# One core, a two-block network with 16 experts: layer 1's memory keys ahead of the experts, the memory's norm vector in its weights, expert products interleaved, the overflow branch at the end

## The chip, the cores and the metric

One Trainium2 chip, one core of it. A core has a matrix engine (PE, or TensorE), a vector engine (DVE), an activation engine (ACT), a general engine (POOL, or GpSimd) and a queue engine (SP), which here issues nearly all transfers. The metric is the time of one launch on the device in microseconds (us). Everything is float32, from inputs in HBM to the output in HBM.

## The reference, cut to what matters

```python
# first block: 256 tokens of 1024 features
x = layer_norm(alpha * x + (1 + gt1) * hybrid_mixer(h), ln1_g, ln1_b)
h = layer_norm(x) * (1 + sc2) + sh2
...
# experts: one group of 4 by softmax, the best 2 of its 4 experts
for e in range(16):
    hid = silu(t @ w_gate[e]) * (t @ w_up[e])          # 1024 -> 512
    out = out + gates[:, e:e + 1] * (hid @ w_down[e])  # 512 -> 1024
x = layer_norm(alpha * x + (1 + gt2) * out, ln2_g, ln2_b)
# second block, for l in (0, 1): mixer with w_in, cross-attention, feed-forward
x = x + mixer(rmsnorm(x, norm_mix[l]), ...)
x = x + cross_attn(rmsnorm(x, norm_xattn[l]), rmsnorm(mem, norm_mem[l]), w_xq[l], w_xkv[l], w_xo[l])
x = x + ffn(rmsnorm(x, norm_ffn[l]), ...)

def rmsnorm(x, g): return x * rsqrt(mean(x ** 2) + 1e-6) * g
def cross_attn(hx, hm, w_q, w_kv, w_o):
    q = hx @ w_q
    k, v = hm @ w_kv          # first 512 columns keys, last 512 values
    ...
```

The keys and values of the memory depend on `mem`, `norm_mem[l]` and `w_xkv[l]` alone, so they can be computed anywhere in the program.

## The kernel before, in words

**Products.** Weights stream from HBM in blocks of 1 MB into a ring of 6 buffers (`raw`, L114 to L117). For most products a block is then split into a high part `whi` (ACT, L140) and a low part `wlo` (DVE, or another engine that the list `loeng` names, L140 and L141), in rings `hi` and `lo` of 4 half-blocks each, and `mm3` (L163 to L165) makes three matmuls of each pair. `linA` gives tokens by features in `psA` (128x512 matmuls), `linB` features by tokens in `psB` (128x256). `featT` (L228, L249) transposes an activation on PE and splits it, on ACT (high) and DVE (low). Expert products take their weights unsplit, as single matmuls.

**Memory.** `memT(l)` (L1720) loads `mem_2`, normalises it (`normT`, L296: multiply by the row's factor `memr` and by the vector `gn` on DVE, L294), and transposes it. `keys(l)` (L1734) and `values(l)` (L1741) multiply with the two halves of `w_xkv_2[l]`. Where they stand in the program: keys(0) at the very start (L445), values(0) within the router (L1185), keys(1) behind the last expert (L1304), values(1) as `filler` between the layer norm at the experts' end and the second block.

**Router and dispatch.** From x, PE, DVE and ACT compute the logits, the chosen experts and each token's rank in its expert (`moe`, L1083; logits and ranks to L1181). Each expert has 64 slots. The gathers (L1191 to L1196) bring the tokens into slot order with 128x512 matmuls.

**Experts.** They are taken in 8 pairs q (L1258 to L1295). For a pair, `half(q, 0)` and `half(q, 1)` (matmul at L1244) make gate and up into one PSUM bank each, the two experts on 64 partitions each; `hid` is formed on ACT and DVE (L1273, L1274), transposed on PE (`pth`, L1283), copied to SBUF by ACT (`hx`, L1285) and multiplied with the down weights (`yg`, L1292). PE's order in a pair is: gate, up, the combine of the pair before (L1375 to L1383: `evac` L1251 on DVE and L228, then `pco` matmuls L1381 and L1382, then an addition into `acc`), the transposes, down. A pair takes 12 weight blocks of 1 MB, 96 in all. The string `CHUNKS` says in which ring each block lands, r for a raw buffer and h for a hi and a lo buffer (the blocks named `wx` in the profile).

**Overflow.** Tokens beyond 64 slots would be handled in a body behind a branch (`overflow`, L1317): every engine loads the count (L1321, TENSOR_LOAD) and branches (L1322). With these inputs the body is skipped. It stands ahead of pair 4.

**Behind the experts** come the last combine with the layer norm's statistics (`lnstat`, L314), `lngb` (the layer norm with gain and bias, L322 to L341; its `rsq` runs on POOL, L257 and L259), the norm and the transposes of x for the second block (L294, L249, L228), and the first products with `w_in_2`.

**Order.** A tile scheduler sets waits from the tiles' use; the order on each engine is that of the program text, except where `with self.after(...)` ties a piece to an instruction.

Of the kernel before, what the change touches and what calls it, by code (L numbers as in the profile page):

```python
# [40 lines left out]
_add("stri", (_i[:, None] < _i[None, :]))  # L41
_add("iota", np.broadcast_to(_i, (P, P)))
# [6 lines left out]
_add("gidx", np.broadcast_to(np.array([0.0, 1.0, 2.0, 3.0]), (P, 4)))  # L49
# [16 lines left out]
class Build:  # L66
    PAGES = {4: 21, 2: 7, 1: 5}
# [99 lines left out]
    def linA(self, x, KT, W, n0, n, r=None, inturn=False, tag="lin"):  # L167
# [5 lines left out]
        for k0 in range(0, KT, kb):  # L173
            kk = min(kb, KT - k0)
            w = self.wblk(W[k0 * P:(k0 + kk) * P, n0:n0 + n].rearrange("(k p) n -> p k n", p=P), kk, n, r)
# [136 lines left out]

    def lnstat(self, st, n, x):
# [77 lines left out]
    def attn(self, qk, V, out, first=True, nsink=None, gate=None, swa=False):  # L391
# [4 lines left out]
        mk = lambda m, n: m.rearrange("p (a b) -> p a b", a=4)[:, 0:n, :]  # L396
        PTs = {}
        for i, heads in ((0, (0, 1, 2, 3)), (1, (0, 1)), (1, (2, 3))):
# [4 lines left out]
            if swa and i == 1:  # L403
                nc.tensor.matmul(S[:, :, 0:P], self.identb, self.smaskb.rearrange("p (a b) -> p a b", a=2), start=False, stop=False,
# [33 lines left out]
    def run(self):  # L438
        nc, tc, A = self.nc, self.tc, self.A
        with tc.tile_pool(name="cst", bufs=1) as self.cp, tc.tile_pool(name="w", bufs=2) as self.wp, \  # L440
# [4 lines left out]
            mT = self.memT(0)  # L445
# [22 lines left out]
    def setup(self):  # L468
# [44 lines left out]
    def setup2(self):  # L513
# [6 lines left out]
        self.tri, self.stri, self.iota = self.C("tri"), self.C("stri"), self.C("iota")  # L520
# [30 lines left out]
    def setup3(self):  # L551
        nc, cp = self.nc, self.cp
        mp, rr, r1, rd, d8 = self.late
        b16 = cp.tile([P, 11 * P], BF, name="b16")
        nc.vector.tensor_copy(b16[:, 0:P], self.ident)
        self.identb = b16[:, 0:P]
        o = P
        for i, (m, n) in enumerate((("cmask", 4), ("smask", 2), ("dmask", 4))):
            v = b16[:, o:o + n * P]
            nc.vector.tensor_copy(v.rearrange("p (a b) -> p a b", a=n), bc(mp[:, i * P:(i + 1) * P], 1, n))  # L560
            setattr(self, m + "b", v)
            o += n * P
# [16 lines left out]
    def ropetables(self):  # L579
# [4 lines left out]
        ang = self.small([P, 2, 48], "ang", 1)  # L584
        for t in range(2):
            nc.vector.tensor_scalar(ang[:, t, :], C("invf"), pf[:, t:t + 1], None, op0=ALU.mult)
        k = self.small([P, 2, 48], "kk", 1)
# [11 lines left out]
        sn = self.small([P, 2, 48], "sn", 1)  # L599
# [13 lines left out]
        self.rt = rt  # L613

# [468 lines left out]
    def moe(self):  # L1083
# [174 lines left out]
        for q in range(8):  # L1258
# [8 lines left out]
            elif q < 4:  # L1267
                gather(1, 2 * q - 2)
# [619 lines left out]
```

## Time and profile before

| | us |
|---|---|
| three runs | 1710.87, 1709.19, 1705.22 (median 1709.19) |
| profiled execution | 1710.13, of it span 1708.4 |
| PE busy in the span | 1604.0 (94%) |
| DVE busy | 991.7 (58%) |
| ACT busy | 737.3 (43%) |
| POOL busy | 236.6 (14%) |
| HBM, mean over the span | 198 GB/s |

Times inside the execution are counted from the span's start. In the span, the first mixer ends at about 350 us, the layer norm, router and dispatch last to about 399, the 8 pairs of experts to about 651, and the second block's first product with `w_in_2` begins at about 688. The rows further down are of the views that the prediction uses: the windows view gives for a stretch the busy time of each engine (with the instructions in brackets), the granted clock of TensorE as a share of full speed, the share of time that the transfer engines are busy, and GB/s. The timeline gives start, length, engine, source line, operation, output and inputs; in square brackets stands how long the engine was idle just before and what released it.

### The profile page before, as it was taken

The page shows a single profiled execution, that of the slowest core. Times are in us where ns is not written, and L with a number is a line of the kernel's source. Part 1 is how long each engine was busy: PE and PEld are TensorE (multiplying, and loading weights), DVE is VectorE, ACT ScalarE, POOL GpSimd, SP SyncE. Part 2 cuts the span into 40 slices and gives each one's busy share as a digit, 9 for nine tenths or more (in the row PEclk, how much of TensorE's full clock was granted, in tenths as well). Part 3 has the DMA queues.
Part 4 walks back from the last instruction along what each step waited for, and adds up shares of the span by engine and source line. Part 5 has one row for each costly group of instructions (what it writes and reads, how often), then busy time and mean ns, then how long its engine had stood idle before and what let it go on. Part 6 is the DMA issues. An engine that isn't in the chain of part 4 may idle for free. (4 is left out here: it accounts for less than half of the span.)

```text
span 1708.4 us, 23536 instructions
## 1 busy us (share of the span) xinstructions
PE 1604.0 (94%) x9272; PEld 1258.9 (74%) x9288; DVE 991.7 (58%) x1501; ACT 737.3 (43%) x1282; POOL 236.6 (14%) x262
## 2 busy tenths in 40 slices
PE   6599999988997898999999999999999999999998
PEld 5478988865432336877788789987877787789986
DVE  6857785772211217677746755544777647655544
ACT  3345764432110004565443544444565544544443
POOL 3498442440000002100000000000100000000000
PEclk9699999998998999999999999999999999999999
DMA  9867356645998997544156545654534155535550
GB/s 305 304 198 243 115 167 229 213 165 189 385 403 333 412 415 279 173 129 143 59 173 200 174 131 173 202 179 134 183 93 150 50 189 193 185 116 193 185 185 25
DMA packets 181318, 340.53 MB, mean 199 GB/s; under 512 B 20640, under 2 KB 96528, under 8 KB 173776
## 3 DMA queue, kind: packets, MB, share of 16 engines
q1 hardware_dynamic: 177072, 331.29, 55.9%
q0 software_dynamic: 1936, 6.52, 1.1%
q8 instruction: 76, 1.25, 0.3%
q10 hardware_dynamic: 2192, 1.12, 0.3%
q14 instruction: 42, 0.34, 0.1%
HBM read 337.86 MB, written 1.05 MB: 198 GB/s over the span
## 5 line engine op out<-in xcount | busy, mean ns | idle before, releaser
L141 DVE TENSOR_TENSOR wlo<-raw,whi 128x1024 fp32r<-128x1024 f32 (+3 forms) x368 | 451.5, 1238 | 315.1 <-ACT whi L140 314.3
L140 ACT CAST whi<-raw 128x1024 fp32r<-128x1024 f32 (+3 forms) x372 | 375.1, 1021 | 380.9 <-PE psA L165 148.8
L163 PE MATMUL psB<-hTh,whi 128*128 128x256 f32 x896 | 254.5, 284 | 0.5 <-ACT xbc L883 0.5
L165 PE MATMUL psB<-hTh,wlo 128*128 128x256 f32 x896 | 253.8, 283 | 0.8 <-DVE wlo L141 0.8
L164 PE MATMUL psB<-hTl,whi 128*128 128x256 f32 x896 | 254.2, 284 | 0.0
L163 PE MATMUL psA<-whi,hTh 128*128 128x512 f32 (+4 forms) x496 | 188.1, 380 | 2.6 <-ACT sg L976 1.9
L165 PE MATMUL psA<-whi,hTl 128*128 128x512 f32 (+4 forms) x496 | 187.4, 378 | 0.5 <-DVE hTl L228 0.5
L164 PE MATMUL psA<-wlo,hTh 128*128 128x512 f32 (+4 forms) x496 | 186.6, 376 | 0.0
L163 PEld LDWEIGHTS psB<-hTh,whi 128*128 128x128 f32 x896 | 171.7, 192 | 2.6 <-issue 1.1
L164 PEld LDWEIGHTS psB<-hTl,whi 128*128 128x128 f32 x896 | 171.7, 192 | 2.0 <-issue 1.9
L165 PEld LDWEIGHTS psB<-hTh,wlo 128*128 128x128 f32 x896 | 171.6, 192 | 1.7 <-DVE wlo L141 1.1
L1244 PE MATMUL pgu<-raw,xg 128*64 128x512 f32 x304 | 116.1, 603 | 0.0
L163 PEld LDWEIGHTS psA<-whi,hTh 128*128 128x128 f32 x496 | 93.8, 189 | 20.6 <-ACT sg L976 2.3
L165 PEld LDWEIGHTS psA<-whi,hTl 128*128 128x128 f32 x496 | 93.7, 189 | 18.9 <-issue 2.4
L164 PEld LDWEIGHTS psA<-wlo,hTh 128*128 128x128 f32 x496 | 93.7, 189 | 16.0 <-issue 0.7
L1244 PE MATMUL pgu<-wx,xg 128*64 128x512 f32 x208 | 94.9, 599 | 0.0
L363 ACT ACTIVATE pr<-S,nm 128x256 f32<-128x256 f32 (+1 forms) x160 | 66.4, 427 | 59.7 <-DVE nm L356 41.8
L638 POOL TENSOR_TENSOR macc<-macc,wmod 128x512 f32<-128x512 f32 x59 | 91.8, 1557 | 1.8
L164 PE MATMUL pd<-wlo,hhl 128*128 128x512 f32 x176 | 69.8, 397 | 0.0
L165 PE MATMUL pd<-whi,hhl 128*128 128x512 f32 x176 | 69.6, 395 | 0.0
L163 PE MATMUL pd<-whi,hhl 128*128 128x512 f32 x176 | 69.3, 395 | 0.0
L274 POOL TENSOR_SCALAR sse<-ssq 128x1 f32<-128x1 f32 x16 | 3.9, 242 | 443.8 <-ACT xn L272 432.1
(580 smaller groups left out, 3006.4 us busy)
## 6 DMA issues: line engine op xcount, KB each, us to landing
raw<-in_w_in SPq DMA_DIRECT2D x62, 1024.0 KB, 5.2
raw<-in_w_gate_up SPq DMA_DIRECT2D x44, 1024.0 KB, 5.1
raw<-in_w_down SPq DMA_DIRECT2D x42, 1024.0 KB, 6.1
wmod<-in_w_mod SPq DMA_DIRECT2D x48, 512.0 KB, 5.0
raw<-in_w_gate SPq DMA_DIRECT2D x19, 1024.0 KB, 8.3
raw<-in_w_up SPq DMA_DIRECT2D x19, 1024.0 KB, 10.5
wx<-in_w_gate SPq DMA_DIRECT2D x26, 512.0 KB, 8.7
wx<-in_w_up SPq DMA_DIRECT2D x26, 512.0 KB, 12.3
```

Of the source, the lines that this page charges most:

```text
L140: self.wsplits.append((self.nc.scalar.copy(hi, rv), self.loeng.pop(0).tensor_sub(lo, rv, hi.bitcast(F32)) if self.loeng else self.nc.vecto ...
L141: self.nc.vector.tensor_sub(lo, rv, hi.bitcast(F32))))
L163: m(out, l[0], r[0], start=start, stop=False)
L164: m(out, l[0], r[1], start=False, stop=False)
L165: self.lastmm = m(out, l[1], r[0], start=False, stop=stop)
L274: self.nc.gpsimd.tensor_scalar(sq[2], sq[1][:, 0:1], 1.0 / D, RMS_EPS, op0=ALU.mult, op1=ALU.add)
L363: le = nc.scalar.activation(pr[:, h, :], S[:, h, :], AF.Exp, bias=nm[:, h:h + 1], accum_out=den[:, h:h + 1])
L638: return e.tensor_add(acc, acc, w)
L1244: self.lastmm = nc.tensor.matmul(ps[i * 64:i * 64 + 64, :], x, w[i][k], start=kt == 0, stop=kt == 7, skip_group_check=True)
```

## The change

**Keys of layer 1.** `keys(1)` now stands right behind `values(0)`, before the first expert, on the same transposed memory; `loeng` is now DVE, DVE and four times POOL, so that four low parts run on POOL in place of two. At the end only `values(1)` is left as filler, and its weights are loaded and split ahead of the branch.

**Norm vector.** `memT` multiplies the memory by the row factor only (`scaledT`: one DVE operation per 128 rows). The vector `norm_mem` is loaded as a column, and `wblk` multiplies the raw weight block by it, block of 128 rows by block, on ACT and in place, ahead of the split.

**Experts.** `half` now makes half of a gate or up product. The next pair's first gate half goes in front of this pair's transposes, the second between `hx` and the down product. The gathers and `slots` for later pairs move with them. `CHUNKS` is now "rrrrrrhhhh".

**Branch.** The overflow branch is now behind the last combine, ahead of `values(1)` and the layer norm. Its body, if taken, recomputes the statistics.

**Small parts.** The rank uses `tri` in place of `stri`, the iota is 64 wide, the masks are kept once and broadcast in the matmul's operand, temporaries of the rope tables and of the softplus lie in pages, and one page more is reserved (`PAGES`).

```diff
-    def wblk(self, src, a, b, r=None, pages=None):
+    def wblk(self, src, a, b, r=None, pages=None, gain=None):
         r = self.raw(src, a, b) if r is None else r
+        if gain is not None:
+            for j in range(a):
+                self.nc.scalar.activation(r[:, j * b:(j + 1) * b], r[:, j * b:(j + 1) * b], AF.Copy, scale=gain[:, j:j + 1])
...
+    def scaledT(self, x, r, name):
+        xT = self.newT(8, name)
+        self.chain = []
+        for t in range(2):
+            self.nc.vector.tensor_scalar(x[t], x[t], r[t], None, op0=ALU.mult)
+            self.featT(x[t], 8, xT, t)
+            self.f(x[t])
+        return xT
...
+        nc.scalar.dma_start(cr[8:24, 0:P], A["norm_mem_2"].rearrange("l (a b) -> (l a) b", b=P))
...
-        nc.tensor.transpose(pt[:, 0:8], cr[0:8, 0:P], idt[:8, :8])
+        nc.tensor.transpose(pt[:, 0:24], cr[0:24, 0:P], idt[:24, :24])
+        self.memg = cp.tile([P, 16], F32, name="memg")
+        nc.scalar.copy(self.memg, pt[:, 8:24])
...
-    CHUNKS = "rrhrh"
+    CHUNKS = "rrrrrrhhhh"
...
-        self.loeng = [nc.vector, nc.vector, nc.gpsimd, nc.gpsimd]
+        self.loeng = [nc.vector, nc.vector] + [nc.gpsimd] * 4
         self.values(0, self.mT0)
+        self.keys(1, self.mT0)
...
-        late, ready = None, []
+        late = None
+        pg = self.bank("lin", "pg")
+        for c in range(2):
+            half(0, 0, c, pg)
+        slots(0)
         for q in range(8):
             if q == 4:
                 self.f(*Sp, *xh, *xl, *xgp[0])
-                ready += [[self.wchunk(wgu(0, 8 + i, c)) for i in range(2)] for c in range(2)]
-                self.overflow(oi, gov, acc)
-            pg = half(q, 0)
...
-            pu = half(q, 1)
-            if late:
-                self.combine(ST[(q - 1) // 4][:, (q - 1) % 4, :], evac(late), acc)
+            pu = self.bank("lin", "pu")
+            for c in range(2):
+                half(q, 1, c, pu)
             hid = self.a(2, "hid")
             nc.scalar.activation(hid, pg, AF.Silu)
             nc.vector.scalar_tensor_tensor(hid, hid, gs[:, q:q + 1], pu, op0=ALU.mult, op1=ALU.mult)
...
+            if late:
+                self.combine(ST[(q - 1) // 4][:, (q - 1) % 4, :], evac(late), acc)
+            if q < 7:
+                pg = self.bank("lin", "pg")
+                half(q + 1, 0, 0, pg)
             pt = v4(self.bank("m", "pth"))
...
             nc.scalar.copy(v4(hx), pt)
...
+            if q < 7:
+                half(q + 1, 0, 1, pg)
             y = [self.bank("S", f"yg{n}") for n in range(2)]
...
         with self.after(self.lastraw):
-            mT = self.memT(1)
-            w = self.wB(8, A["w_xkv_2"][1], 0)
+            mT = self.memT()
+            wv = self.wmem(1, 0, 512) + self.wmem(1, 1, 512)
         self.combine(ST[1][:, 3, :], evac(late), acc, st)
...
-        self.keys(1, mT, w)
+        self.overflow(oi, gov, acc, st)
 
         def filler():
-            self.values(1, mT)
+            self.values(1, mT, wv)
             self.freeT(mT)
```

The order of instructions shows at three places what this moves. On POOL, between the first mixer and the experts (`rsv` and `rs` are the layer norms' reciprocal roots, for which the scaling on DVE waits; `wlo` the low weight parts; the last rows are the router's), the order before was:

```order
L257 TENSOR_SCALAR rsv<-bmv 128x1
L259 TENSOR_TENSOR rs<-rsv,mhalf 128x1
L140 TENSOR_TENSOR wlo<-raw,whi 128x1024 x2
L257 TENSOR_SCALAR rsv<-bmv 128x1 x2
L259 TENSOR_TENSOR rs<-rsv,mhalf 128x1 x2
L1228 TENSOR_SCALAR acc_3460<-x_269 128x1024
L1116 TENSOR_TENSOR xnl_3175<-xn,xnh_3173 128x1024
L257 TENSOR_SCALAR rsv<-bmv 128x1
```

and with the change, where lines 138, 259 and 261 are the former 140, 257 and 259:

```order
L259 TENSOR_SCALAR rsv<-bmv 128x1
L261 TENSOR_TENSOR rs<-rsv,mhalf 128x1
L138 TENSOR_TENSOR wlo<-raw,whi 128x1024 x2
L259 TENSOR_SCALAR rsv<-bmv 128x1 x2
L138 TENSOR_TENSOR wlo<-raw,whi 128x1024
L261 TENSOR_TENSOR rs<-rsv,mhalf 128x1 x2
L138 TENSOR_TENSOR wlo<-raw,whi 128x1024
L259 TENSOR_SCALAR rsv<-bmv 128x1
L261 TENSOR_TENSOR rs<-rsv,mhalf 128x1
L1124 TENSOR_TENSOR xnl_3178<-xn,xnh_3176 128x1024
L1124 TENSOR_TENSOR xnl_3179<-xn,xnh_3177 128x1024
```

One low part has come between the second `rsv` and its `rs`, and one more ahead of the next `rsv`. On PE, from the end of up (`pgu`) to the start of down in a pair of experts, before:

```order
L1244 MATMUL pgu<-wx,xg_3407 64x512
L1244 MATMUL pgu<-raw,xg_3408 64x512
L1244 MATMUL pgu<-wx,xg_3408 64x512
L1244 MATMUL pgu<-raw,xg_3408 64x512
L1244 MATMUL pgu<-wx,xg_3408 64x512
L1283 MATMUL pth<-idt,hid 128x128 x4
L1292 MATMUL yg_6226<-raw,hx 64x512
L1292 MATMUL yg_6227<-raw,hx 64x512
```

and with the change (`pu` is this pair's up, `pg` the next pair's gate):

```order
L1251 MATMUL pu<-raw,xg_3556 64x512 x4
L1251 MATMUL pg<-wx,xg_3553 64x512
L1288 MATMUL pth<-idt,hid 128x128 x4
L1251 MATMUL pg<-wx,xg_3553 64x512 x3
L1251 MATMUL pg<-wx,xg_3554 64x512 x4
L1251 MATMUL pg<-wx,xg_3555 64x512 x4
L1251 MATMUL pg<-wx,xg_3556 64x512 x4
L1303 MATMUL yg_4320<-raw,hx 64x512
L1303 MATMUL yg_4321<-raw,hx 64x512
```

Nothing stood between up, the transposes and down; now one gate matmul stands ahead of the transposes and 15 ahead of down. On PE at the experts' end (`pco` is the last combine, `ptr` the transposes of the memory, `psB` keys(1)), before:

```order
L1381 MATMUL pco<-yh,ST_3459 128x512
L249 MATMUL ptr<-idt,xn 128x128 x8
L1381 MATMUL pco<-yh,ST_3459 128x512
L1382 MATMUL pco<-yl,ST_3459 128x512 x2
L249 MATMUL ptr<-idt,xn 128x128 x8
L163 MATMUL psB<-memTh_6388,whi 128x256
L164 MATMUL psB<-memTl_6389,whi 128x256
L165 MATMUL psB<-memTh_6388,wlo 128x256
```

and with the change:

```order
L1396 MATMUL pco<-yh,ST_3607 128x512
L251 MATMUL ptr<-idt,xn 128x128 x8
L1396 MATMUL pco<-yh,ST_3607 128x512
L1397 MATMUL pco<-yl,ST_3607 128x512 x2
L251 MATMUL ptr<-idt,xn 128x128 x8
L1396 MATMUL pco<-yh,ST_3607 128x512
L1397 MATMUL pco<-yl,ST_3607 128x512
L1396 MATMUL pco<-yh,ST_3607 128x512
L1397 MATMUL pco<-yl,ST_3607 128x512
L1333 TENSOR_LOAD oi
L1334 COMPARE_AND_BRANCH
```

Where keys(1) began there is now the branch, once the last combine is through, and values(1) begin behind it. On DVE the branch stands between the statistics of the last layer norm and their aggregate (L322 before), with one low part of a weight block behind it ahead of that; on SP the loads of the memory, of two blocks of `w_xkv_2`, of the gain and bias and of the first two blocks of `w_in_2` stand ahead of it.

## Rows read from the trace of the kernel before

**Rows 1.** Waits of PE, 398.7 to 650.7 us: total us, times, longest us.

```profile
PE pth L1283 <- DVE hid L1274: 5.6, 6, 0.9
PE yg L1292 <- ACT hx L1285: 4.1, 6, 0.7
PE pco L1382 <- issue: 3.0, 1, 3.0
```

**Rows 2.** Timeline of PE and DVE around the branch.

```profile
526.92 0.59 PE L1292 MATMUL yg<-wx,hx 128*64 128x512 f32 x1
...
532.26 1.22 PE L1381 MATMUL pco<-yh,ST 128*128 128x512 f32 x2 [4.75 <-ACT yh L228]
...
530.79 1.29 DVE L1251 TENSOR_TENSOR yf<-yg,gt 128x512 f32<-128x512 f32 x2 [11.90 <-PEq L1322]
```

**Rows 3.** Windows: us, busy of PE, PEld, DVE, ACT, POOL, PEclk, DMA share, GB/s.

```profile
527.50:541.00 13.50, 5.80 (x10) 2.12 (x9) 4.13 (x7) 1.14 (x2) 0.63 (x1) 0.67 1.02 414
541.00:650.70 109.70, 100.38 (x424) 35.70 (x423) 20.34 (x32) 8.37 (x14) 0.00 (x0) 0.98 0.99 397
...
540.00:560.00 20.00, 18.38 (x76) 6.25 (x76) 2.12 (x3) 1.18 (x2) 0.00 (x0) 0.93 0.86 322
...
600.00:620.00 20.00, 18.41 (x84) 6.37 (x86) 1.49 (x3) 1.18 (x2) 0.00 (x0) 1.00 1.02 416
```

**Rows 4.** SP's queue: first expert block behind ten prefetched ones, and the last.

```profile
408.81 1.17 SPq L117 DMA_DIRECT2D raw<-in_w_down  x2
...
631.10 0.33 SPq L117 DMA_DIRECT2D raw<-in_w_down  x1
```

**Rows 5.** Timeline of PE: a pair's down product.

```profile
616.17 3.66 PE L1292 MATMUL yg<-raw,hx 128*64 128x512 f32 x16 [0.68 <-ACT hx L1285]
```

**Rows 6.** Windows: the layer norm, router and gathers ahead of the experts.

```profile
350.00:398.70 48.70, 36.47 (x174) 29.89 (x172) 32.96 (x75) 13.48 (x22) 18.00 (x14) 0.83 0.41 147
```

**Rows 7.** Timeline of POOL and DVE at the first layer norm.

```profile
356.25 5.14 POOL L140 TENSOR_TENSOR wlo<-raw,whi 128x1024 fp32r<-128x1024 f32 x2
...
356.23 5.71 DVE L341 SCALAR_TENSOR_TENSOR x<-sg,rs,l1b 128x512 f32<-128x512 f32 x2 [0.47 <-POOL rs L259]
...
370.56 1.40 DVE L341 SCALAR_TENSOR_TENSOR x<-sg,rs,l1b 128x512 f32<-128x512 f32 x2
```

**Rows 8.** Timeline of PE: first and last of 46 matmuls in a row within keys(1).

```profile
667.73 0.28 PE L165 MATMUL psB<-memTh,wlo 128*128 128x256 f32 x1
...
672.98 0.28 PE L165 MATMUL psB<-memTh,wlo 128*128 128x256 f32 x1
```

**Rows 9.** Timeline of PE: last down product, first matmul of the second block.

```profile
650.15 0.59 PE L1292 MATMUL yg<-raw,hx 128*64 128x512 f32 x1
...
687.55 0.34 PE L163 MATMUL psA<-whi,hTh 128*128 128x384 f32 x1
```

**Rows 10.** Timeline of DVE between these two.

```profile
663.96 1.28 DVE L314 BATCH_NORM_STATS2 bst<-acc 128x6 f32<-128x512 f32 x2
...
667.41 0.27 DVE L322 BATCH_NORM_AGGREGATE bmv<-bst 128x2 f32<-128x12 f32 x2
...
674.28 1.22 DVE L141 TENSOR_TENSOR wlo<-raw,whi 128x1024 fp32r<-128x1024 f32 x1
...
676.30 1.42 DVE L294 SCALAR_TENSOR_TENSOR xn<-x,rr,gn 128x512 f32<-128x512 f32 x2 [0.80 <-POOL rr L284]
...
682.17 1.28 DVE L228 TENSOR_TENSOR hTl<-ptr,hTh 128x512 fp32r<-128x512 f32 x2
```

**Rows 11.** Timeline of the program's start.

```profile
11.18 2.74 DVE L294 SCALAR_TENSOR_TENSOR xn<-xn,memr,gn 128x512 f32<-128x512 f32 x4 [10.18 <-POOL memr L284]
...
27.55 1.28 ACT L809 ACT_TABLE_LOAD   x1
...
48.02 3.15 PE L624 MATMUL psmod<-ones,macc 128*128 128x1 f32 x14 [6.71 <-DVE macc L640]
```

**Rows 12.** Groups by shape, engine ACT: busy us, mean ns, idle before.

```profile
L1509 ACT COPY qm<-psA 128x256 f32<-128x256 f32 x8 | 3.0, 371 | 1.9 <-PE psA L165 1.9
```

More of the change, by code (lines that the diff above doesn't have):

```diff
@@ L403, in attn @@
             if swa and i == 1:
-                nc.tensor.matmul(S[:, :, 0:P], self.identb, self.smaskb.rearrange("p (a b) -> p a b", a=2), start=False, stop=False,
+                nc.tensor.matmul(S[:, :, 0:P], self.identb, bc(self.smaskb, 1, 2), start=False, stop=False,
                                  skip_group_check=True)
@@ L583, in ropetables @@
         nc.vector.tensor_copy(pf, self.pi)
-        ang = self.small([P, 2, 48], "ang", 1)
+        page = self.a(2, "rtmp")
+        ang, k, sn = [page[:, i * 96:(i + 1) * 96].rearrange("p (a b) -> p a b", a=2) for i in range(3)]
         for t in range(2):
             nc.vector.tensor_scalar(ang[:, t, :], C("invf"), pf[:, t:t + 1], None, op0=ALU.mult)
-        k = self.small([P, 2, 48], "kk", 1)
         MAGIC = 12582912.0
@@ L613, in ropetables @@
         self.rt = rt
+        self.f(page)
     def modps(self, j, n, acc, late=False):
@@ L789, in mixer1 @@
         nc.vector.tensor_scalar(z[:, :, 16:24], z[:, :, 16:24], -1.0, None, op0=ALU.mult)
-        az = self.small([P, 2, 24], "az", 1)
+        page = self.a(1, "spt")
+        az, e, w, w2, pl = [page[:, i * 48:(i + 1) * 48].rearrange("p (a b) -> p a b", a=2) for i in range(5)]
         nc.vector.scalar_tensor_tensor(az, z, -1.0, z, op0=ALU.mult, op1=ALU.max)
-        e = self.small([P, 2, 24], "e", 1)
         nc.scalar.activation(e, az, AF.Exp, scale=-1.0)
-        w = self.small([P, 2, 24], "w", 1)
         nc.vector.tensor_scalar(w, e, 2.0, None, op0=ALU.add)
@@ L808, in mixer1 @@
         nc.vector.scalar_tensor_tensor(sp, pl, 2.0, z, op0=ALU.mult, op1=ALU.add)
+        self.f(page)
         nc.scalar.activation(self.Aneg, self.alog, AF.Exp)
@@ L1234, in moe, with half @@
         wdn = lambda e, c: W[2][e].rearrange("(p j) n -> p j n", j=4)[:, 2 * c:2 * c + 2, :]
-        def half(q, j):
-            ps = self.bank("lin", "pgu")
-            for c in range(2):
-                w = ready.pop(0) if ready else [self.wchunk(wgu(j, 2 * q + i, c)) for i in range(2)]
-                for k in range(4):
-                    kt = 4 * c + k
-                    for i in range(2):
-                        x = xg[q // 4][kt // 2][:, kt % 2, q % 4 * P + i * 64:q % 4 * P + i * 64 + 64]
-                        self.lastmm = nc.tensor.matmul(ps[i * 64:i * 64 + 64, :], x, w[i][k], start=kt == 0, stop=kt == 7, skip_group_check=True)
-            return ps
+        def half(q, j, c, ps):
+            w = [self.wchunk(wgu(j, 2 * q + i, c)) for i in range(2)]
+            for k in range(4):
+                kt = 4 * c + k
+                for i in range(2):
+                    x = xg[q // 4][kt // 2][:, kt % 2, q % 4 * P + i * 64:q % 4 * P + i * 64 + 64]
+                    nc.tensor.matmul(ps[i * 64:i * 64 + 64, :], x, w[i][k], start=kt == 0, stop=kt == 7, skip_group_check=True)
         def evac(y):
@@ L1373, in overflow @@
             self.f(*hT)
+            for t in range(2):
+                for n in range(2):
+                    self.lnstat(st[t], n, acc[t])
     def combine(self, ST, y, acc, st=None):
```

82 lines of the change are left out of this document (38 added, 44 removed).

## The prediction, made before the changed kernel ran

> **What bounds the kernel now.** I read the table first, then PE's waits in the expert stage, the windows of that stage, SP's queue, and last the timelines where the change cuts in: the branch, the front of the stage and its end. The span is 1708.4 us and PE is busy for 94% of it, so time can only come out of PE's idle time, or out of PE work that runs at the lower clock. The stage from 398.7 to 650.7 us has three kinds of it. At each pair's transposes PE waits for `hid`, 0.9 us, and ahead of down for `hx`, 0.7 [rows 1]; each was recorded 6 times in 8. At the branch PE ends its down product at 527.5 and gets going only at 532.3, and again stands for 2.95 that no other engine explains [rows 1, 2]; DVE came through at 530.8. From 527.5 to 541.0 PE is busy for 5.8 of 13.5 us at a mean clock of 0.67 [rows 3], between the two levels of 1.2 and 2.4 GHz. The third thing to see there is that PE never waits for a weight. The transfers run at 416 GB/s where buffers are free, but fall to 322 between 540 and 560 [rows 3], because PE frees the buffers too late. Both must be counted: PE's stalls, and how soon the transfers become the limit once these are gone.
>
> **The experts.** What PE itself needs: the stage of 252.0 us, less the pairs' waits, 8 x (0.9 + 0.7) = 12.8, less the branch. Of the branch's 13.5 us, 5.8 were work at the lower clock, which is 2.9 at the higher, so 10.6 go. PE's work would end at 650.7 - 12.8 - 10.6 = 627.3. Both savings are likely to be real: the new order on PE puts a gate matmul ahead of the transposes and 15 of them ahead of down, and DVE and ACT need under a microsecond for `hid` and `hx`.
>
> What the weights need: 96 blocks of 1.0486 MB are 100.7 MB. Ten blocks fit the rings and are loaded before the stage; SP then issues the next at 408.8 [rows 4]. The other 90.2 MB at 416 GB/s [rows 3] take 217 us. Behind that I put 8 us, an estimate: 3.7 for the matmuls of the last down product [rows 5] and some 4 for the last block's landing and for a few gaps. So the last product ends no sooner than 408.8 + 217 + 8 = 634 by the weights, against 627 by PE: the weights become the bound, PE starts to wait for them, and 7 of the 23 us that its stalls cost are not won. A pair shows the same: 12 blocks at 416 GB/s need 30.2 us, and PE, which took 109.7 / 4 = 27.4 [rows 3], would need 25.8. The new `CHUNKS` changes only which ring a block lands in; both patterns hold ten blocks, so it gets nothing. Bounds: if the last 4 us shrink away, the stage ends at 630; if the rate is the 397 GB/s that 541.0 to 650.7 shows [rows 3], the weights need 227 us and it ends at 644. The last block was issued at 631.1 before [rows 4], which a restart at 408.8 and a rate of 416 without gaps would bring to some 626.
>
> **The front.** Keys(1) are 96 matmuls. They take (672.98 - 667.73) / 45 = 0.117 us each in a row [rows 8], so 11.2 us. From 350.0 to 398.7 PE is idle for 48.7 - 36.5 = 12.2 us [rows 6], in which they nearly fit, since they depend on the memory alone. They add 16 scalings of a 128x256 block on ACT at 0.37 us [rows 12], 5.9, and the values 8 larger ones; ACT is busy for 13.5 of 48.7 us there, so I cost them at nothing. If that cover goes, the splits, and with them keys(1), are late by up to that much. On POOL, two low parts more come ahead of a layer norm's `rs`. A low part takes 5.14 / 2 = 2.57 us, and while two of them ran, two DVE additions took 5.71 us, against 1.40 for the same two later [rows 7]. One of the two new ones lies between `rsv` and `rs`, where DVE waits. Bounds: -2 (a PE that is busy there holds the higher clock for the gathers, mean clock before 0.83 [rows 6]) and +7.7 (three times 2.57, a lock included). I take +2, one low part less a little of the clock. Everything in the expert stage moves with it: E, the end of the last down product, goes from 634 to 636, against 650.7: **-14.8**, front included.
>
> The Trainium skill, page "SBUF — State Buffer", section "SBUF: two separate sides", says that a DVE operation with two SBUF inputs and a GpSimd operation that reads SBUF take a shared port pair exclusively, for a whole instruction, and the loser stands still. The trace agrees, with 5.71 against 1.40 us. By that rule both new low parts hold up DVE, for 5.1 us, and the sum would be 3.1 us higher.
>
> **The end of the stage.** Before, the last down product ended at 650.74 and the second block's first matmul came at 687.55, 36.8 us later [rows 9]; keys(1) and values(1) filled that time on PE, 11.2 us each. Now there is only values(1), so the chain on DVE is what counts. From E to the end of the statistics: 665.24 - 650.74 = 14.5 [rows 10]. Then the branch: from PE's last product to DVE's first operation behind it 530.79 - 527.51 = 3.3 [rows 2]. One low part that now stands ahead, 1.2. From the aggregate to `xn`, 676.30 - 667.41 = 8.9, and from `xn` to the last `hTl`, 683.45 - 676.30 = 7.2 [rows 10]. Together 35.1, which is -1.7 against 36.8. PE's values, 11.2 us, lie under this if they run at the higher clock. Against it: the skipped body, and a PE that stood idle at the branch and starts at the lower clock. I take **+2**, between -1.7 and +20 (the rivals below).
>
> **The start.** The memory's norm on DVE is 4 operations of 2.74 us together [rows 11], and 2 wider ones with one input now; rope tables leave the start too. ACT gets 16 scalings, 5.9 us, and a table load of 1.28 [rows 11, 12]. PE's last wait there is 6.7 us for `macc` on DVE [rows 11], so DVE is what counts: **-1**, between -3.5 (the norm's 2.74 and a little of the tables) and +3 (half of ACT's). Rank, masks, iota and pages cost nothing: they lie beside other work, and removed PE columns and DVE copies can only help by tenths.
>
> **The sum.** 1710.1 - 14.8 + 2 - 1 = 1696.3, from the profiled execution; the median of the runs shown is 0.9 lower. I say 1696. A difference of 0.3%, 5.1 us, is about what a measurement of this kernel can tell from no change.
>
> **The rivals.**
> - *A, more is won:* no gaps at the last blocks (-4), a tail that ends with the chain (-1.7 in place of +2), and a start at its lower bound (-3.5). For it: the two chains on DVE and SP have room. Against it: each is a lower bound. 1710.1 - 18.8 - 1.7 - 3.5 = 1686; half way 1690. Chance 0.11.
> - *C, the branch makes the tail dear on PE.* PE reaches values(1) at E + 14.5 + 3.3 + 2.95 (the stall seen behind the branch [rows 1]) = 20.8 at worst, and runs them at 1.2 GHz, 22.4 us, with the transposes behind them and `hTl` still to come, 1.3: E + 44.5, 7.7 over 36.8. 1710.1 - 14.8 + 7.7 - 1 = 1702. For it: the clock of 0.67 at the middle branch; against it: PE has little to do before that chain ends, and may start earlier. Chance 0.15. The Trainium skill, page "Runtime: NRT & Kernel Launch", section "Instruction fetch mechanics", says that a taken branch to a target that is not yet fetched stalls for the fetch, and it says so of any engine. The row shows it for PE alone; by the rule DVE would be some 3 us later as well, and the case would be 1705.
> - *E, the stage does not do what the change says:* waits for weights replace the waits for `hid`, at 397 GB/s. E is 646 and the time 1710.1 - 4.7 + 2 - 1 = 1706. For it: that window; against it: it holds the hole at 540 that came from the branch. Chance 0.09.
> - *D, slower:* the branch keeps its full price of 13.5 us, now with nothing beside it, and values(1) run behind it on PE at the lower clock, ahead of the transposes: 14.5 + 13.5 + 22.4 + 7.2 = 57.6, which is 20.8 over 36.8. 1710.1 - 14.8 + 20.8 - 1 = 1715. It decides if PE has run less than about a third of values(1) when `xn` is ready. Against it: DVE was through the middle branch after 3.3 us. Chance 0.08.
>
> **How the numbers follow.** My forecast has 0.57, with 1689 to 1703 as its own range. The range reaches to A's lower end and past E: 1686 to 1710; only D and little more lies outside. Faster by over 5.1 us (under 1704): the forecast almost whole, 0.55, A, and half of C, 0.74. Within: the rest of both and E, 0.18. Slower: D, 0.08.
>
> **What would show it.** Right: no wait of PE at the transposes or ahead of down, but waits for `raw` and `wx`; transfers at 414 to 418 GB/s without a hole from some 411 to 630; the last down product ending near 636; DVE held for 3 us at the end's branch; the second block's first product some 38 us after E; low parts ahead of `rs` on POOL. Wrong: a stage that ends behind 644; a gap of over 45 us between the last down product and the second block; experts that begin later than 403.

## The result, and the profile after

The changed kernel takes 1717.95 us (median of 4 runs, 1715.82 to 1721.02), the kernel before 1707.40 beside it (4 runs). The ratio is 1.0061, with a 95% interval of 1.0036 to 1.0086. Forecast were 1696 us, 1686 to 1710, with a chance of 0.08 for slower: the forecast is wrong, in its sign too.

```profile
span 1714.0 us, 23559 instructions
...
PE 1611.0 (94%) x9288; PEld 1264.0 (74%) x9288; DVE 979.5 (57%) x1491; ACT 760.2 (44%) x1332; POOL 238.2 (14%) x262
```

The page's head says only that PE is as busy as before. What helps is to cut the span at four events which both traces show, and to set the forecast beside each piece. The events are the layer norm's first aggregate ahead of the experts (DVE), the first gather matmul (PE), the end of the last down product (E, on PE), and the second block's first matmul (PE).

| us | before | after | difference | forecast |
|---|---|---|---|---|
| start, to the first aggregate | 353.1 | 360.2 | +7.1 | -1 |
| front, aggregate to first gather | 38.1 | 51.9 | +13.8 | +2 |
| stage, first gather to E | 259.5 | 242.7 | -16.9 | -16.8 |
| tail, E to second block | 36.8 | 36.2 | -0.6 | +2 |
| the rest | 1020.9 | 1023.0 | +2.1 | 0 |
| span | 1708.4 | 1714.0 | +5.6 | -13.8 |

(The forecast for the stage is its -14.8 less the +2 that it held for the front.) The experts gained what was forecast, to 0.1 us. Two pieces ahead of them lost 20.9.

**The stage.** The last pair and the tail on PE, from its timeline (start us, us, engine, line, operation, idle time before it):

```profile
646.22 0.75 PE L1288 MATMUL pth<-idt,hid 128*128 128x128 f32 x4 [0.84 <-DVE hid L1276]
647.65 7.14 PE L1303 MATMUL yg<-raw,hx 128*64 128x512 f32 x32 [0.68 <-ACT hx L1290]
...
674.04 0.77 PE L165 MATMUL psA<-whi,memTh 128*128 128x512 f32 x1 [11.27 <-DVEq L1334]
...
691.01 0.34 PE L165 MATMUL psA<-whi,hTh 128*128 128x384 f32 x1
```

E is 647.65 + 7.14 = 654.79. PE's waits from 430 to 655 us answer to [rows 1]; the stall of 3.0 at the middle branch is gone, the waits for `hx` are down from 6 to 1, but those for `hid` are still there in 4 pairs:

```profile
PE pco L1396 <- ACT yh L230: 3.5, 6, 0.6
PE pth L1288 <- DVE hid L1276: 3.4, 4, 0.8
PE pco L1396 <- DVE acc L1398: 2.9, 5, 0.7
...
PE yg L1303 <- ACT hx L1290: 0.7, 1, 0.7
```

The order that was built on PE differs from pair to pair. Ahead of the transposes, 16 matmuls of the next pair's gate stand in the first two pairs, and two behind up in the next two. In the fifth and sixth pair two are mixed with the last of up, and in the seventh and eighth there is none; these four wait. The first and the fifth pair:

```profile
441.10 3.65 PE L1251 MATMUL pg<-wx,xg 128*64 128x512 f32 x16
444.68 0.75 PE L1288 MATMUL pth<-idt,hid 128*128 128x128 f32 x4
...
562.06 0.59 PE L1251 MATMUL pg<-wx,xg 128*64 128x512 f32 x1
563.49 0.75 PE L1288 MATMUL pth<-idt,hid 128*128 128x128 f32 x4 [0.84 <-DVE hid L1276]
```

The windows answer to [rows 3]; the hole of 322 GB/s between 540 and 560 is gone, but one of 355 stands at 500 to 520:

```profile
440.00:460.00 20.00, 20.00 (x99) 8.84 (x100) 3.48 (x7) 4.44 (x8) 0.00 (x0) 1.00 1.02 407
500.00:520.00 20.00, 19.46 (x95) 7.56 (x95) 1.15 (x4) 2.61 (x5) 0.00 (x0) 1.00 0.92 355
540.00:560.00 20.00, 18.79 (x82) 6.29 (x80) 5.24 (x8) 1.83 (x3) 0.00 (x0) 1.00 1.01 405
600.00:620.00 20.00, 17.71 (x70) 5.88 (x68) 5.99 (x9) 1.52 (x3) 0.00 (x0) 1.00 1.02 416
```

PE nowhere waits for `raw` or `wx`. SP's queue shows why (restart of the expert blocks, and the last of them):

```profile
425.50 1.17 SPq L115 DMA_DIRECT2D raw<-in_w_gate  x2
...
629.39 4.17 SPq L115 DMA_DIRECT2D raw<-in_w_down  x4
```

The last block is issued by 633.6, and E comes 21 us later; before it was 19 us [rows 4, 9]. What SP waits for in 400 to 660 us are mostly PE's products (the two largest rows), so PE paces the weights and not the other way round:

```profile
SPq L115 <- PE pg L1251: 40.3, 15, 11.6
SPq L115 <- PE pu L1251: 40.1, 13, 6.3
```

**The start.** PE's waits from 0 to 357 us begin with one that the trace before does not have (`macc` are the sums of the modulation, `psmod` the product that takes them):

```profile
PE psmod L696 <- POOL macc L648: 9.1, 1, 9.1
```

**The front.** POOL's timeline, with the two low parts that are new (375.00 and 378.40) around the second `rs`:

```profile
373.37 1.55 POOL L259 TENSOR_SCALAR rsv<-bmv 128x1 f32<-128x1 f32 x2 [4.87 <-DVE bmv L334]
375.00 2.42 POOL L138 TENSOR_TENSOR wlo<-raw,whi 128x1024 fp32r<-128x1024 f32 x1
377.37 1.09 POOL L261 TENSOR_TENSOR rs<-rsv,mhalf 128x1 f32<-128x1 f32 x2
378.40 2.51 POOL L138 TENSOR_TENSOR wlo<-raw,whi 128x1024 fp32r<-128x1024 f32 x1
```

and DVE's beside it:

```profile
373.09 0.26 DVE L334 BATCH_NORM_AGGREGATE bmv<-bst 128x2 f32<-128x12 f32 x2
...
377.97 3.50 DVE L353 SCALAR_TENSOR_TENSOR x<-sg,rs,l1b 128x512 f32<-128x512 f32 x2 [3.37 <-POOL rs L261]
...
382.58 0.79 DVE L344 TENSOR_SCALAR xn<-x,bmv,rs 128x1024 f32<-128x1024 f32 x1
```

The second aggregate is at 373.09, and `xn` comes 9.5 us behind it: 2.4 for a low part ahead of `rs`, then two additions on DVE that take 3.50 us while POOL forms the next low part, and only then `xn`. Before, `xn` stood ahead of the two additions. The first gather is at 412.11.

**The tail.** DVE's timeline answers to [rows 10]:

```profile
667.47 1.23 DVE L139 TENSOR_TENSOR wlo<-raw,whi 128x1024 fp32r<-128x1024 f32 x1
...
673.99 1.23 DVE L139 TENSOR_TENSOR wlo<-raw,whi 128x1024 fp32r<-128x1024 f32 x1 [5.29 <-DVEq L1334]
...
683.69 1.42 DVE L296 SCALAR_TENSOR_TENSOR xn<-x,rr,gn 128x512 f32<-128x512 f32 x2 [0.80 <-POOL rr L286]
```

DVE is held for 5.29 us at the branch, PE for 11.27 (above). PE then runs values(1) at the lower of its two levels, but only for the first 6 us, as the granted clock of two windows shows (0.53, then 1.00):

```profile
674.00:680.00 6.00, 5.96 (x15) 4.73 (x16) 5.28 (x8) 0.59 (x2) 3.94 (x5) 0.53 0.87 257
680.00:691.00 11.00, 10.01 (x51) 7.80 (x50) 8.70 (x13) 7.25 (x16) 3.29 (x6) 1.00 0.13 28
```

The last `hTl` on DVE ends at 690.65 and the last matmul of the values at 691.2: chain and PE come out together, and the second block starts 36.2 us behind E.

### The profile page after: what moved, and what is told of

It is laid out like the page before. It is cut to its first block, busy times and chain, and to the rows that moved or that the text cites. A ratio compares the mean times of both kernels' runs of the same rounds, so it can differ in the third digit from the quotient of the medians.

```text
span 1714.0 us, 23559 instructions
## 1 busy us (share of the span) xinstructions
PE 1611.0 (94%) x9288; PEld 1264.0 (74%) x9288; DVE 979.5 (57%) x1491; ACT 760.2 (44%) x1332; POOL 238.2 (14%) x262
## 3 DMA queue, kind: packets, MB, share of 16 engines
q8 instruction: 75, 1.23, 0.3%
## 4 chain that ended last, share of the span: by engine, by line
PE 55%; DVE 2%; issue 1%; ACT 1%; POOL 1%; POOLq 0%; DVEq 0%; ACTq 0%
PE psA L167 8%; PE psA L165 8%; PE psA L166 8%; PE psB L166 4%; PE psB L167 4%; PE psB L165 4%; PE pd L166 2%; PE pd L167 2%; PE pd L165 2%; PE S L438 2%; PE tp L394 1%; PE ptr L251 1%; PE psA L214 1%; PE psA L212 1%; PE psA L213 1%
## 5 line engine op out<-in xcount | busy, mean ns | idle before, releaser
L648 POOL TENSOR_TENSOR macc<-macc,wmod 128x512 f32<-128x512 f32 x59 | 85.7, 1455 | 1.5
L1257 DVE TENSOR_TENSOR yf<-yg,gt 128x512 f32<-128x512 f32 x16 | 11.0, 690 | 101.9 <-PE yg L1303 101.9
L647 POOL TENSOR_SCALAR wmod<-wmod,cact 128x512 f32<-128x512 f32 x59 | 62.3, 1064 | 23.5 <-DMA wmod<-in_w_mod 23.5
```

What stands on the lines that cost most here:

```text
L647: e.tensor_scalar(w, w, c, 1.0, op0=ALU.mult, op1=ALU.mult)
L648: return e.tensor_add(acc, acc, w)
```

## The experiments

Each kernel is the changed one with the edit shown. The cuts are those of the table above; rest and span are from the profiled execution, time is the median of all runs. Runs of different rows were on different chips, so times are compared by their ratio to the kernel before on the same chip.

| us | start | front | stage | tail | rest | span | time | ratio to before (95%) |
|---|---|---|---|---|---|---|---|---|
| before | 353.1 | 38.1 | 259.5 | 36.8 | 1020.9 | 1708.4 | 1707.40 | 1 |
| the change | 360.2 | 51.9 | 242.7 | 36.2 | 1023.0 | 1714.0 | 1717.95 | 1.0061 (1.0036 to 1.0086) |
| e1_modord | 363.0 | 49.9 | 242.7 | 36.1 | 1023.1 | 1714.8 | 1720.44 | 1.0087 (1.0070 to 1.0104) |
| e2_pool2 | 365.9 | 41.9 | 242.6 | 35.7 | 1023.2 | 1709.3 | 1710.23 | 1.0027 (1.0009 to 1.0045) |
| e3_kend | 362.6 | 37.7 | 246.0 | 45.4 | 1022.8 | 1714.6 | 1716.61 | 1.0061 (1.0044 to 1.0078) |
| e4_mid | 364.2 | 48.0 | 248.6 | 24.8 | 1026.1 | 1711.6 | 1712.29 | 1.0033 (1.0019 to 1.0048) |
| e5_late | 355.2 | 49.9 | 244.5 | 35.5 | 1023.5 | 1708.6 | 1709.44 | 1.0010 (0.9991 to 1.0029) |
| e6_front_mid_late | 352.2 | 43.1 | 250.2 | 25.2 | 1025.8 | 1696.4 | 1695.76 | 0.9924 (0.9904 to 0.9943) |
| e7_gate | 353.7 | 41.7 | 246.8 | 25.3 | 1025.8 | 1693.3 | 1695.72 | 0.9941 (0.9919 to 0.9963) |
| e8_chunks | 353.0 | 42.9 | 249.4 | 23.9 | 1026.8 | 1696.0 | 1698.89 | 0.9947 (0.9932 to 0.9962) |
| e9_no_pool | 351.0 | 42.4 | 246.3 | 23.9 | 1027.0 | 1690.5 | 1693.14 | 0.9919 (0.9892 to 0.9946) |

The same code at the start gave 360.2 to 365.9 in the kernels that have the extra page there from the first microsecond, and the same front 48.0 to 51.9; a few us between two of these rows mean nothing.

### The start: POOL's order, or the page?

Why does PE wait 9.1 us for POOL? POOL's timeline of the change:

```profile
128.24 1.80 POOL L647 TENSOR_SCALAR wmod<-wmod,cact 128x512 f32<-128x512 f32 x2 [9.33 <-DMA wmod<-in_w_mod]
...
137.25 4.89 POOL L648 TENSOR_TENSOR macc<-macc,wmod 128x512 f32<-128x512 f32 x3
...
156.08 3.70 POOL L648 TENSOR_TENSOR macc<-macc,wmod 128x512 f32<-128x512 f32 x3
```

POOL stands 9.33 us for a modulation block, with additions of blocks that are there behind it. A wait of that length is not new. The kernel before has this one:

```profile
134.66 0.69 POOL L635 TENSOR_SCALAR macc<-wmod,cact 128x512 f32<-128x512 f32 x1 [9.18 <-DMA wmod<-in_w_mod]
```

What is new is that the sums come too late for PE. That could be POOL's order, where multiplications run ahead of additions, or the blocks' arrival. The first experiment ties each multiplication to the addition before it:

```diff
+                    with self.after(*self.lastadd):
-                    self.macc(self.nc.gpsimd, acc[...], w[...], kb * 2 + k, kb == 0 and k == 0)
+                        self.lastadd = [self.macc(self.nc.gpsimd, acc[...], w[...], kb * 2 + k, kb == 0 and k == 0)]
```

> The changed kernel, with one thing more: on POOL each multiplication of a modulation weight block is followed by its addition, where the changed kernel runs 9 multiplications ahead of their additions. Theory A (the order on POOL: the additions stand queued behind a multiplication that waits for a transfer): PE's wait of 9.1 us for the modulation sums at 150 to 160 us falls under 2 us, the first layer norm's aggregate comes at some 353 instead of 360.2 us, and the time falls by 6 to 9 us, to some 1709. Rival B (the transfers or POOL's own speed set the end of these sums): the wait stays over 6 us, the time within 2 us of the changed kernel's.

POOL then waited longer, and PE too. POOL's timeline of this kernel:

```profile
131.91 1.21 POOL L648 TENSOR_SCALAR wmod<-wmod,cact 128x512 f32<-128x512 f32 x1 [22.14 <-DMA wmod<-in_w_mod]
```

and PE's:

```profile
165.37 1.58 PE L698 MATMUL psmod<-ones,macc 128*128 128x1 f32 x6 [10.89 <-POOL macc L649]
```

The order isn't it: POOL stood for a block from 109.8 to 131.9, and the start stayed at 363.0. What is left is when a block is loaded, and blocks are loaded into pages. The change has 22 pages in place of 21, and each request takes the next free one, so that from the first request on every block gets another page, which is free at another time. The second experiment withholds the 22nd page until the router, where `keys(1)` needs it:

```diff
     def __init__(...):
...
+        self.free[4].pop()
...
     def moe(self):
+        self.free[4].append(21)
```

> The changed kernel with one thing else: the 22nd large page is kept out of use until the router begins, so that the modulation weights go through the same 21 pages as before, and POOL's order of multiplications and additions is that of before again; nothing else on POOL is forced. Theory A (the added page changes POOL's order, additions stand queued behind a multiplication whose block is late): PE's wait of 9 to 11 us for the modulation sums falls under 3 us, the first aggregate comes at 349 to 355 us in place of 360.2, time 6 to 10 us lower. Rival B (an earlier start only waits longer for sums whose transfers come when they come): the wait stays over 6 us, time within 3 us.

PE's timeline of that kernel shows the product as in the kernel before (157.13 there), with no wait:

```profile
157.04 1.56 PE L697 MATMUL psmod<-ones,macc 128*128 128x1 f32 x6
```

The first aggregate moves to 355.2 and the ratio from 1.0061 to 1.0010, by 8.7 us. All five kernels with the page withheld start at 351.0 to 355.2, all five that have it at once at 360.2 to 365.9. The means are 353.0 and 363.2, so the page costs some 10 us: shown. That it does so through the time at which a page comes free was not tried; it is an inference from the program and from POOL's waits for blocks.

### The front: low parts on POOL, or the keys?

```diff
-        self.loeng = [nc.vector, nc.vector] + [nc.gpsimd] * 4
+        self.loeng = [nc.vector, nc.vector] + [nc.gpsimd] * 2
```

> The changed kernel with two low parts on POOL in place of four; the others of keys(1) go to DVE. Theory A (the low parts ahead of the layer norm's rs on POOL hold up DVE): from the second layer norm's aggregate to its xn 3 to 5 us in place of 9.5, first gather 5 to 7 us earlier, time 4 to 7 us lower. Rival B (keys(1) hold up the router wherever their low parts run, by PE's and ACT's order): first gather within 2 us, time within 2 us.

DVE's timeline of that kernel:

```profile
378.71 0.27 DVE L334 BATCH_NORM_AGGREGATE bmv<-bst 128x2 f32<-128x12 f32 x2
...
382.50 0.81 DVE L344 TENSOR_SCALAR xn<-x,bmv,rs 128x1024 f32<-128x1024 f32 x1 [1.24 <-POOL rs L261]
383.22 1.41 DVE L353 SCALAR_TENSOR_TENSOR x<-sg,rs,l1b 128x512 f32<-128x512 f32 x2
```

`xn` comes 3.8 us behind the second aggregate in place of 9.5, and stands ahead of the two additions again, which are back at 1.41 from 3.50. The front falls from 51.9 to 41.9, more than expected; the start came out 5.7 later in this execution. The ratio falls by 0.0034 (5.8 us), with intervals that overlap. Over all kernels, the front takes 48.0 to 51.9 with four low parts on POOL (mean 49.9 of 4) and 41.7 to 43.1 with two (mean 42.4 of 4): two low parts cost 7.5 us.

The keys' share of the front comes from the next one, which has two low parts and puts `keys(1)` back to the end:

```diff
-        self.loeng = [nc.vector, nc.vector] + [nc.gpsimd] * 4
+        self.loeng = [nc.vector, nc.vector] + [nc.gpsimd] * 2
         self.values(0, self.mT0)
-        self.keys(1, self.mT0)
...
-            wv = self.wmem(1, 0, 512) + self.wmem(1, 1, 512)
+            wk = self.wmem(1, 0, 256)
...
-            self.values(1, mT, wv)
+            self.keys(1, mT, wk)
+            self.values(1, mT)
```

> The changed kernel with keys(1) back behind the experts, as filler behind the branch together with values(1), and two low parts on POOL; the rest of the change stays. Theory A (keys(1) in the front cost what the front lost): from the first aggregate to the first gather 38 to 40 us in place of 51.9, expert stage as long as in the changed kernel, and from the last down product to the second block 42 to 48 us in place of 36.3: time 2 to 8 us lower. Rival B (the front is late for another reason of the change, such as the scalings on ACT): 48 us or more from aggregate to gather, time 6 or more higher.

The front is 37.7, that of the kernel before. So the keys cost some 4.7 us there (42.4 - 37.7), which the idle time of [rows 6] did not hide whole. Most of it can be read on PE. DVE forms the selection `S`, for which the gathers wait. In the kernel with two low parts and keys in front, keys(1) are not through on PE when its first half is there, and the overflow's count (`pof`), which waits for a later operation on DVE, stands ahead of the gather too:

```profile
403.61 2.36 DVE L1156 TENSOR_TENSOR S<-cst,rr 128x1024 fp32r<-128x1024 f32 x2
406.25 0.28 PE L166 MATMUL psB<-memTl,whi 128*128 128x256 f32 x1
407.37 0.35 PE L1186 MATMUL pof<-of,ones 128*128 128x1 f32 x2 [0.84 <-DVE of L1184]
407.59 0.37 PE L167 MATMUL psB<-memTh,wlo 128*128 128x256 f32 x1
407.79 0.52 PE L1205 MATMUL pga<-S,xnh 128*128 128x512 f32 x1
```

With the keys at the end the gather follows at once:

```profile
399.02 2.36 DVE L1156 TENSOR_TENSOR S<-cst,rr 128x1024 fp32r<-128x1024 f32 x2
400.30 0.82 PE L1204 MATMUL pga<-S,xnh 128*128 128x512 f32 x1 [1.76 <-DVE S L1156]
```

The gather comes 4.2 us behind the start of `S` in all four kernels with two low parts and keys in front, and 1.3 here and in the kernel before: 2.9 of the 4.7 us are what now stands on PE ahead of the first gather.

At the end the keys cost more: the tail is 45.4 against 35.7, the stage 246.0 against 242.6, and the ratio 1.0061 against the 1.0027 of two low parts with keys in front. So the time did not fall by the 2 to 8 us that were expected: what the front won, the end lost. With the branch at the end, moving the keys was right, and is worth some 6 us; the two intervals just touch.

Can the chain do without POOL? In the last kernel no low part runs there; it holds the edits of e7_gate (below) and:

```diff
-        self.loeng = [nc.vector, nc.vector] + [nc.gpsimd] * 2
+        self.loeng = []
```

> As e7, with no low part on POOL at all: all six run on DVE. Theory A (any low part on POOL ahead of rs or beside two-input work on DVE costs more than DVE's own 1.2 us): aggregate to gather 36 to 39 us in place of 41.7, time 2 to 5 us lower than e7's. Rival B (what is left of the front's loss is keys(1) on PE and ACT): aggregate to gather within 1.5 us of e7's, time within 2 us.

DVE's timeline has `xn` 11.6 us behind the first aggregate (at 351.0), where it was 16.6 with two low parts (382.50 - 365.9):

```profile
362.59 0.81 DVE L345 TENSOR_SCALAR xn<-x,bmv,rs 128x1024 f32<-128x1024 f32 x1 [1.51 <-POOL rs L262]
```

but the first gather comes 42.4 behind the aggregate as with two. The router's last product ends 2.4 us sooner behind the aggregate than in e7_gate (29.3 against 31.7), and the gather comes 13.1 us behind that and not 9.9: what the layer norm gains, the routing behind it gives back. Of these 3.2 us, 1.8 lie ahead of `S`, where DVE now forms a low part among the router's small operations, and 1.4 between `S` and the gather, where more of keys(1) is left. The time is 2.6 us below that of e7_gate, with intervals that overlap, and the start of the profiled execution is 2.7 shorter: a gain is not shown.

### The end: where is the branch cheapest?

This kernel puts the branch back to the fifth pair, and keeps the rest. The pipeline of gate products is interrupted there once: the pair's gate product stands behind the branch, its weights are loaded ahead of it.

```diff
             if q == 4:
                 self.f(*Sp, *xh, *xl, *xgp[0])
+                pre = [[self.wchunk(wgu(0, 8 + i, c)) for i in range(2)] for c in range(2)]
+                self.overflow(oi, gov, acc, None)
+                pg = self.bank("lin", "pg")
+                for c in range(2):
+                    half(4, 0, c, pg, pre[c])
...
-            if q < 7:
+            if q < 7 and q != 3:
...
-        self.overflow(oi, gov, acc, st)
```

> The changed kernel with the overflow branch back ahead of pair 4, the first two gate products of that pair loaded ahead of it and made behind it; the rest stays. Theory A (the branch costs less at the end): the expert stage is 9 to 13 us longer, the tail 4 to 6 us shorter (DVE is held for 5.3 us there), time 4 to 8 us higher. Rival B (a branch costs the same in both places): expert stage longer by 9 to 13, tail shorter by as much, time within 2 us.

Neither theory holds. The stage is 5.9 longer, but the tail 11.4 shorter, since values(1) now starts 8 us behind E (654.70 + 6.03 = 660.73) and not 19. PE's timeline:

```profile
548.97 1.04 PE L1251 MATMUL pg<-wx,xg 128*64 128x512 f32 x2 [2.76 <-PEq L1338]
...
654.70 6.03 PE L1308 MATMUL yg<-raw,hx 128*64 128x512 f32 x22
...
669.11 1.22 PE L165 MATMUL psA<-whi,memTh 128*128 128x512 f32 x2
...
685.53 0.44 PE L165 MATMUL psA<-whi,hTh 128*128 128x384 f32 x1 [0.68 <-ACT hTh L230]
```

Not all of that counts: the second block's first matmul now runs while the second half of the tokens is still in the layer norm, and the rest is 3.1 longer. From the first gather to the end of the span, kernels with the branch at the end take 1301.5 to 1303.5 (the change, e1, e2, e5; mean 1302.2), those with it in the middle and without the edit of e7_gate below 1299.5 to 1301.2 (e4, e6, e8; mean 1300.3). So by the profiles the place of the branch is worth some 2 us, and it is the middle that is cheaper: what its move to the end gains in the stage is given back behind it. By the ratios e4 is 0.0028 below the change, with intervals that overlap, so the times alone do not show it.

### All of it together

Two low parts, the page withheld, the branch in the middle: the edits of e2, e4 and e5.

> The changed kernel with three things together: two low parts on POOL in place of four, the branch back ahead of pair 4, the 22nd page kept out of use until the router. Theory (the three losses are apart and add up): aggregate at 349 to 355, 42 us from there to the first gather, 248 to 250 to the last down product, 25 to 27 to the second block: it begins at 664 to 674 where the kernel before has 687.5, time 1688 to 1698. Rival (the page's cost is not its order, e5): second block at 672 to 680, time 1695 to 1702.

The time is 1695.76 us, 0.9924 of the kernel before (0.9904 to 0.9943): faster than both kernels. Between the two profiles 16.8 of the 17.6 us lie in the start and the front, that is with the page and the two low parts; the branch's place has the rest. `keys(1)` in front, the norm vector in the weights and the pipelined products are left in. That the time equals the forecast of the change (1696) is chance: against the kernel before, the front is 5.0 us longer and not 2, the stage 9.3 shorter and not 16.8, the tail 11.6 shorter and not 2 longer, and the rest 4.9 longer.

### Is PE or the weights the stage's bound?

On top of e6, the transposes are tied behind the first half of the next pair's gate product, so that a gate matmul always covers `hid`:

```diff
-                    nc.tensor.matmul(ps[...], x, w[i][k], ...)
+                    self.lasth = nc.tensor.matmul(ps[...], x, w[i][k], ...)
...
-            for k in range(4):
-                nc.tensor.transpose(...)
+            with self.after(self.lasth):
+                for k in range(4):
+                    nc.tensor.transpose(...)
```

> As e6, and the transposes of each pair are tied behind the first gate half of the next pair, which the changed kernel's PE order had in the first pairs only (one matmul or none in the last five). Theory A (PE is the bound of the stage and the remaining waits for hid of 0.8 us cost their full time): no wait of PE at the transposes but for pairs 3 and 7, stage 3 to 5 us shorter than e6's, time 2 to 5 us lower. Rival B (the weights are the bound, and PE then waits for them): stage within 1 us of e6's, time within 1.5 us.

PE's waits from 395 to 690 us of e6 have

```profile
PE pth L1295 <- DVE hid L1283: 4.3, 5, 0.9
```

and of this kernel

```profile
PE pth L1296 <- DVE hid L1283: 1.7, 2, 0.9
```

The two that are left are the pair ahead of the branch and the last one, which have no gate product to put there. The stage is 3.4 us shorter (246.8 against 250.2), where weights as the bound would have left it as it was. The two kernels with this edit have 246.8 and 246.3, the three with the branch in the middle and without it 248.6 to 250.2. So by the profiles PE is the bound; the weights have little room left, since the transfers ran at over 400 GB/s in most windows. The times, expected to fall by 2 to 5 us, don't tell the two kernels apart: 1695.72 and 1695.76, on intervals of 0.2%.

The other edit to the weights' path sets the pattern of the rings back, on top of e6:

```diff
-    CHUNKS = "rrrrrrhhhh"
+    CHUNKS = "rrhrh"
```

> As e6, with the string that names the rings of the expert blocks set back to rrhrh. Theory A (both strings hold ten blocks, so the string is worth nothing): gather to last down product within 2 us of e6's 250.2, time within 2 us of e6's. Rival B (blocks that come in runs of one ring give a part of the stage's gain): stage 3 us or more longer.

The stage takes 249.4 against 250.2, and the ratio's interval (0.9932 to 0.9962) overlaps that of e6. The new pattern is worth nothing that these runs can tell, as forecast.

The kernel e9 above, with the gate tied and no low part on POOL, has the lowest time of all: 1693.14 us, 0.9919 of the kernel before (0.9892 to 0.9946). Its interval has no overlap with that of the change, but it overlaps those of e6, e7 and e8.

## Why the prediction was wrong

**The front: the step that failed most.** "I take +2, one low part less a little of the clock", between -2 and +7.7. It was +13.8 in the profile, and +11.8 by the mean of four. Two things are in it. The low parts alone cost 7.5 us, about the upper bound for the whole front; 5.7 of it stand up to `xn` (9.5 against 3.8). Not one held up DVE, but both: the first because it stood on POOL ahead of `rs`, the second because it slowed the two additions, and these stood ahead of `xn`. The order of instructions showed one low part between `rsv` and `rs` and another behind; which DVE operations run beside the second was not read. And the keys themselves, costed at nothing under 12.2 us of PE's idle time, cost 4.7. Idle time in a window is no promise that work fits into it ahead of the next event: 2.9 of the 4.7 are the rest of keys(1), and `pof` among it, that PE had in front of the first gather when the first half of `S` was there. Where the other 1.8 go was not tried.

The Trainium skill, page "SBUF — State Buffer", section "SBUF: two separate sides", says that of a DVE operation with two SBUF inputs and a GpSimd operation that reads SBUF one stands still for the whole instruction of the other; by that rule the sum was to be 3.1 higher. The trace agrees with it, 3.50 against 1.41 us, but only for the second low part: while POOL formed the first, DVE waited for `rs`. The two cost 5.7 up to `xn` and 7.5 in all, not 5.1.

**The start: the second step that failed.** "Rank, masks, iota and pages cost nothing: they lie beside other work". With the page at hand from the start, PE waited 9.1 us for the modulation sums: -1 became +7.1, and some 10 over the kernels that differ in the page. No view of the trace before could price that. But the bounds were set on the norm and ACT alone, and a resource from which all buffers are dealt was given no bound at all. Nor is the -1 to be seen: the five kernels without the page start at 353.0 in the mean, the kernel before at 353.1. One PE product early on (`pc`) comes 5.9 us sooner in the change (78.12 against 84.06), but nothing of it reaches the first aggregate.

**The stage: right in size, not in its reason.** Forecast were 242.8 us from the first gather to E, measured 242.7. But the reason was "the weights become the bound", with "waits for `raw` and `wx`", and there are none: SP waits for PE, and removing PE's waits shortened the stage by 3.4. The other bound, PE at 627.3, took all waits for `hid` away, by an order that was read for one pair. In the last four pairs the transposes have two gate matmuls mixed into up, or none, to cover the wait, and 0.84 us each remain. The combine waits for `acc` 2.9 us in place of 1.8. The 225 us from SP's restart to E came out as 229.3 (654.79 - 425.50) from a restart that was 17 late. That both came out near each other is chance.

**The tail: inside its bounds, by parts that made up for each other.** Forecast were 38.8 us, a chain of 35.1 and 3.7 on top for the skipped body and PE's lower clock; measured 36.2. DVE was held for 5.29 us and not 3.3, and a second low part stands beside the branch (1.23), but the statistics ended 1.9 sooner behind E, and the chain came to 35.9. Of rival C the first half came true: PE began values(1) at E + 19.3 (C had 20.8 "at worst") at the lower level (0.53). But it rose after 6 us, so that the values, with the transposes among them, took 17 us and not 22.4, and ended with the chain and not 8 us behind it. The Trainium skill, page "Runtime: NRT & Kernel Launch", section "Instruction fetch mechanics", says that an engine stalls at a taken branch whose target is not yet fetched; the prediction's estimate from that was a DVE some 3 us later. It was 2.0 later (5.29 - 3.3); that fetching was the cause, no run here shows.

**The rivals.** The one that ended slower (D, 1715) gave about the measured time, by a mechanism that didn't occur (a tail of 57.6). The losses came from terms held at nothing or next to it, and no rival was made of them.

**Open.** The 2.1 us in the rest remain in all later kernels (1.9 to 2.6 in those with the branch at the end) and weren't tested.

## What to carry to other kernels

- A buffer pool's size is an edit to every transfer that draws on it: if a page is needed late, add it late, and bound what a new rotation can do at the places where the program waits for a transfer.
- Before work is put into an engine's idle time, look at which chain that time is waiting for, and what of the new work (its scalings, splits and low parts too) runs on that chain's engines. A low part on POOL near a layer norm's `rs` costs its own length and what it slows on DVE.
- When a large change comes out slower, cut the span at events that both traces show: four cuts told here that the expert stage gained and that two side edits ate it.

## What the runs showed of the hardware that was not expected

- A low part on POOL beside DVE additions with two operands in SBUF: two additions took 3.50 us against 1.41, and the chain lost 7.5 us to two low parts of 2.5 each.
- A branch behind the last combine held DVE for 5.29 us, and PE's first matmul behind it came after 11.27 idle us; within the expert loop (e4_mid) PE stood 2.76. By the profiles the two places differ by about 2 us in sum. PE's granted clock was 0.53 in the first 6 us behind the branch at the end, and 1.00 after that.
- 405 to 418 GB/s were sustained in nine of the ten windows of 20 us from 440 to 640 us (355 in the tenth) with PE busy for 17.7 to 20 of 20 us, and PE did not wait for a weight.
